# Three spacing constants and the place of the background work changed in a hybrid attention, convolution and pooling trunk on one core

## The chip, the cores and the metric

The kernel runs on one core of one Trainium2 chip. The metric is device time in microseconds (us); lower is better. A time is that of one execution; where several runs are given, the median counts.

## The reference, cut to what matters

One layer over a sequence of 2048 tokens with 1024 channels, in float32:

```
h   = rmsnorm(x) * g1;  p = h @ W_in
A   = banded attention: 8 heads x 64, chunks of 64 tokens, each with the 8 chunks before it,
      q and k normalised per head, a learned bias by clipped distance, softmax
B   = gb * conv3_causal(gc * hin)                 (256 channels)
C   = (mean over the last 2/4/8/16 tokens - u), a 64x64 map per group, a scale   (256 channels)
x   = x + concat(A, B, C) @ W_out
h2  = rmsnorm(x) * g2
x   = x + relu(h2 @ W1)^2 @ W2                    (4096 hidden)
```

## The kernel before

The tokens are worked in four blocks of 512 (`block(b)`), and after them comes the MLP over two halves of 1024 tokens, which the change does not touch. A float32 product is made of three TensorE passes (`mm3`, lines 179 to 182) over a high and a low part of each operand; the parts of a weight tile are made by `Weights.split` (cast on ScalarE or GpSimd, rest on VectorE, lines 160 and 161). All loads and stores are issued by SyncE (SP).

A block has these stages in this order on TensorE:

- `project(0)`, `project(1)`, `project(2)`: q, k and v. Each has eight steps `k` of 12 matmuls. `project(0)` also loads the block's x (`load_x`) and the rows for the first norm (`row_power`, into tiles tagged `sv`, four buffers, squared by `look_rows`). Within `project(2)`, at the steps listed in `EARLY`, k is normalised and the first pair of heads is prepared by `prep(0)`: transposes, splits, a store of k to memory (`kd`) and loads of `kx`, `qs` and `qx` for each head, partly from on-chip memory to on-chip memory. The first scores of the attention (lines 601 and 602) need these loads.
- the attention, woven with side work. `weave` takes `attention` as its main stream and a side stream. A main step is half of a unit (a head and 128 queries): either the scores, or the transposes of one unit and the values of another. There are 68 main steps. After each main step `RATE` side steps fall due (`RATE0` in block 0). The first thing that `attention` yields is `LEAD`, before any instruction of its own, so that about `LEAD * RATE` side steps stand before the first scores.

The side stream (`side`) is the output projection of the block before (`outproj`, 32 steps of 6 matmuls; eight output groups of 4 steps), and then the convolution and pooling (`convpool`, 32 steps, also 6 matmuls each, in groups `dense(g)` of 4 steps that each fill one of the two PSUM banks tagged `d`). Block 0 has only the latter. Into the first steps of `convpool` are set those of `stats`, the second norm of the block before: `token_cols` sums the squares per token after three steps, then some steps pass, then `rsqrt_steps` (11 small VectorE operations, lines 200 to 207) and `row_bcast` (line 256: eight matmul passes into a bank tagged `d`, which spread the result over all partitions), a copy and a store to `r2d`.

A third, background stream is `chores`: first `survey`, 64 steps, each of which loads two tiles of 256 KB of the MLP's weights into `sv` buffers and squares two earlier ones on ScalarE; then, from block 3's `project(1)` on, `early_operands`, 28 steps, which load x of the first two blocks from memory (`x2d`), scale it, form sums, cast it and store it (`xd`). One chore step is taken at set places of the projections, and `CHORES[b]` of one per side step (`pace`).

The order of TensorE's instructions within a weave is fixed as written (`InOrder`). The order on the other engines and on SP's queue is chosen when the kernel is built, by a planner that goes by its own estimates of times, by order in the program and by free buffers; instructions of `attention` go before others of the same neighbourhood (`AHEAD`). An engine works through its list in that order, and waits where the next one is not ready.

Of the kernel before, what the change touches and what calls it, by code (L numbers as in the profile page):

```python
# [33 lines left out]

C_G1, C_G2, C_QG, C_KG, C_CW, C_PS, C_FB = 0, 8, 16, 17, 18, 24, 26
NCOL = 34
RATE, RATE0 = 0.95, 0.45
AHEAD = 1500
GAP = 0.0
AHEADW = 2  # L40
# [1 line left out]
RAWN = 3  # L42
TK, TY = 't', 't'
ORDERED = ("PE",)
LEAD = 2
EARLY = (0, 3, 5, 6)
WIN = (2, 4, 8, 16)
SPILLS = (6, 10, 14, 18)
# [44 lines left out]
def trunk(ctx, tc, xT, xN, cols, cinv, w_qkv, w_cp, w_out, w1, w1t, w2, nbias, pool_w, outT):  # L93
# [16 lines left out]
    def pd(name, tag="d"):  # L110
        if tag == "d":
            return psd.tile([P, 512], F32, tag="d", name=name)
        return psa.tile([P, 512], F32, tag=tag, bufs=3 if tag == "t" else 1, name=name)

    def pbig(name, tag):
        return psa.tile([P, 2, 512], F32, tag=tag, bufs=1, name=name)
# [26 lines left out]
    class Weights:  # L143
# [20 lines left out]
        def next(self):  # L164
            while len(self.ready) <= min(self.used, AHEADW):
                if not self.raws:
                    self.load()
                if not self.raws:
                    break
                self.split()  # L170
                while len(self.raws) < min(self.used + 1, RAWN):
                    n = len(self.raws)
                    self.load()
                    if len(self.raws) == n:
                        break
            self.used += 1
            return self.ready.pop(0)

    def mm3(out, ah, al, bh, bl, start, stop):
        te.matmul(out, ah, bh, start=start, stop=False)  # L180
        te.matmul(out, ah, bl, start=False, stop=False)  # L181
        anchor.append(te.matmul(out, al, bh, start=False, stop=stop).ins.name)  # L182
# [15 lines left out]
    def rsqrt_steps(pool, a, n, tag):  # L198
        h = pool.tile([P, n], I32, tag=tag + "h", name=tag + "h")
        ve.tensor_scalar(h, a.bitcast(I32), 1, None, op0=ALU.arith_shift_right)  # L200
        r = pool.tile([P, n], F32, tag=tag + "r", name=tag + "r")
        ve.tensor_scalar(r.bitcast(I32), h, -1, 0x5F3759DF, op0=ALU.mult, op1=ALU.add)
        t = pool.tile([P, n], F32, tag=tag + "t", name=tag + "t")
        for _ in range(3):
            ve.scalar_tensor_tensor(out=t, in0=r, scalar=-0.5, in1=r, op0=ALU.mult, op1=ALU.mult)
            ve.tensor_tensor(out=t, in0=t, in1=a, op=ALU.mult)
            ve.scalar_tensor_tensor(out=r, in0=t, scalar=1.5, in1=r, op0=ALU.add, op1=ALU.mult)
        return r
# [36 lines left out]
    def token_cols(acc, name):  # L245
        t = pd(name)
        for i in range(NT):
            te.matmul(t[:, i : i + 1], acc[:, i * P : (i + 1) * P], ones, start=True, stop=True)
        c = sm.tile([P, NT], F32, tag="ms", name=name + "c")
        ve.tensor_scalar(c, t[:, :NT], 1.0 / D, EPS, op0=ALU.mult, op1=ALU.add)  # L250
        return c

    def row_bcast(cs, name):
        t = pd(name)
        for i in range(NT):
            te.matmul(t[:, i * P : (i + 1) * P], cs[:, i : i + 1].broadcast_to([P, P]), ident, start=True, stop=True)
        return t
# [14 lines left out]
    def value_norms(k):  # L272
        raw = scr.tile([P, 512], F32, tag="x", bufs=3, name=f"vw{k}")
        sy.dma_start(raw, w_qkv[2, k])
        g = col[:, C_G1 + k : C_G1 + k + 1]
        q = vacc if k == 0 else scr.tile([P, TB + 16], F32, tag="win", bufs=2, name=f"vq{k}")[:, :TB]
        sc.activation(q, raw, AF.Square, scale=g)
        if k:
            gp.tensor_tensor(out=vacc, in0=vacc, in1=q, op=ALU.add)
# [152 lines left out]
    def block(b, prev_out):  # L432
# [3 lines left out]
        def load_x(k):  # L436
            xr = scr.tile([P, 512], F32, tag="x", bufs=3, name=f"x{b}_{k}")
            sy.dma_start(xr, xT[k * P : (k + 1) * P, t0 : t0 + TB])
            g = col[:, C_G1 + k : C_G1 + k + 1]
            xg = xgs[k]  # L440
            sc.activation(xg[:, 0], xr, AF.Copy, scale=g)
            ve.scalar_tensor_tensor(out=xg[:, 1], in0=xr, scalar=g, in1=xg[:, 0].bitcast(F32), op0=ALU.mult, op1=ALU.subtract)
# [3 lines left out]
        def row_power(n):  # L446
            raw = scr.tile([P, 512], F32, tag="sv", bufs=4, name=f"xn{b}_{n}")
            sy.dma_start(raw, xN[4 * b + n // 2, n % 2])
            return n, raw

        def look_rows(n, raw):
            sc.activation(raw, raw, AF.Square, accum_out=sx[:, n // 2, n % 2 : n % 2 + 1])
# [4 lines left out]
        def project(c, also=lambda k: None):  # L457
            if c != 1:
                big = pbig(f"a{b}_{c}", "s")
                ac = [big[:, 0], big[:, 1]] + [pd(f"a{b}_{c}_{i}", "t") for i in range(2)]  # L460
            else:
                ac = [pd(f"a{b}_{c}_{i}", "dydt"[i]) for i in range(4)]
            rows = []
            for k in range(KT):
                if c == 0:
                    load_x(k)
                if c == 0:
                    rows.append(row_power(k))
                    if k > 1:
                        look_rows(*rows.pop(0))  # L470
                w = weights.next()
                if b == 0 and c == 1:
                    value_norms(k)
                for i in range(NT):
                    mm3(ac[i], xgs[k][:, 0, i * P : (i + 1) * P], xgs[k][:, 1, i * P : (i + 1) * P], w[:, 0, 0], w[:, 1, 0], k == 0, k == KT - 1)
                also(k)
                if b and c and k % 2:
                    next(chore, None)
            for r in rows:
                look_rows(*r)  # L480
            return ac

        acq = project(0)
        rstd, epsq = [], sm.tile([P, NT], F32, tag="epsq", name=f"epsq{b}")

# [71 lines left out]
        if b == NB - 1:  # L557
            early_open.append(True)
        ack = project(1)
        nrm["q"] = normalize(acq, "q")  # L560
        if b == 0:
# [9 lines left out]

        steps = early()
        acv = project(2, lambda k: next(steps) if k in EARLY else None)
        R = p1.tile([P, TB], F32, tag="acc", name=f"R{b}")
        vr = sm.tile([P, NT], F32, tag="vr", name=f"vr{b}")
# [77 lines left out]
        def attention(first):  # L653
            ready = first
            yield LEAD if b else LEAD * RATE / RATE0
            scored = flipped = done = None
# [148 lines left out]
        def stats():  # L805
            for _ in range(3):
                yield
            ms2 = token_cols(acc2, f"ms2_{b}")
            for _ in range(4):
                yield  # L810
            r2 = rsqrt_steps(sm, ms2, NT, "r1")
            rb2 = row_bcast(r2, f"rb2{b}")
            r2s = po.tile([P, 512], F32, tag="sq", bufs=1, name=f"r2s{b}")
            sc.copy(r2s, rb2)
            sy.dma_start(r2d[b], r2s)
            yield
# [244 lines left out]
    for n, u in enumerate(units):  # L1061
        kind, tb, c, i = u
# [86 lines left out]
```

## Time and profile before

| what | value |
|---|---|
| median of 3 runs | 2141.82 us (2135.64 to 2143.37) |
| the profiled execution | 2138.21 us |
| its span, from the first to the last instruction | 2136.3 us |
| TensorE (PE) busy | 2041.8 us, 96% of the span |
| VectorE (DVE) busy | 1337.3 us, 63% |
| ScalarE (ACT) busy | 1016.4 us, 48% |
| GpSimd (POOL) busy | 575.8 us, 27% |
| moved by DMA | 399.69 MB, mean 187 GB/s |

TensorE is busy for nearly the whole span; the other engines are not. The stages up to the MLP take about the first 960 us. Matmul ends are modelled, so what is sure in the profile is when TensorE stands idle and what ended the wait. The granted clock (PEclk) has two levels in this profile: 1.0 is 2.4 GHz, 0.5 is 1.2 GHz.

In the rows further down, a row of busy time by stretch holds the stretch and its length, then the busy time (and number of instructions) of PE, PEld, DVE, ACT and POOL, the granted clock, the busy share of the DMA engines and GB/s. A row of a timeline holds start, duration, engine, line, operation and tiles, and in brackets how long the engine stood idle before it, and what ended that.

### The profile page before, as it was taken

The page shows a single profiled execution, that of the slowest core. Times are in us where ns is not written, and L with a number is a line of the kernel's source. Part 1 is how long each engine was busy: PE and PEld are TensorE (multiplying, and loading weights), DVE is VectorE, ACT ScalarE, POOL GpSimd, SP SyncE. Part 2 cuts the span into 40 slices and gives each one's busy share as a digit, 9 for nine tenths or more (in the row PEclk, how much of TensorE's full clock was granted, in tenths as well). Part 3 has the DMA queues.
Part 4 walks back from the last instruction along what each step waited for, and adds up shares of the span by engine and source line. Part 5 has one row for each costly group of instructions (what it writes and reads, how often), then busy time and mean ns, then how long its engine had stood idle before and what let it go on. Part 6 is the DMA issues. An engine that isn't in the chain of part 4 may idle for free. (4 is left out here: it accounts for less than half of the span.)

```text
span 2136.3 us, 31619 instructions
## 1 busy us (share of the span) xinstructions
PE 2041.8 (96%) x11072; PEld 1257.2 (59%) x11072; DVE 1337.3 (63%) x2208; ACT 1016.4 (48%) x2028; POOL 575.8 (27%) x441
## 2 busy tenths in 40 slices
PE   8999898999999898998999999999999999999999
PEld 6777787887787687764444444444444444444444
DVE  6676466756676677767768779767743053353354
ACT  5466575666564454535656456456143151150330
POOL 1110012000210133154556456446422031130132
PEclk9999999999999999999999999999999999999999
DMA  9676797668854687493465555548733333333344
GB/s 318 195 226 210 225 276 238 203 219 265 269 177 124 194 263 209 156 340 115 166 228 186 182 198 187 183 148 295 250 121 104 101 102 104 99 99 107 101 151 150
DMA packets 219567, 399.69 MB, mean 187 GB/s; under 512 B 26000, under 2 KB 33296, under 8 KB 219408
## 3 DMA queue, kind: packets, MB, share of 16 engines
q1 hardware_dynamic: 219408, 397.68, 58.0%
q8 instruction: 87, 1.43, 0.3%
q14 instruction: 72, 0.59, 0.1%
HBM read 275.42 MB, written 105.38 MB: 178 GB/s over the span
## 5 line engine op out<-in xcount | busy, mean ns | idle before, releaser
L911 PE MATMUL b_d<-ft_u,s_d 128*128 128x512 f16 x1152 | 264.1, 379 | 7.3 <-ACT ft_u L861 3.2
L911 PEld LDWEIGHTS <-s_d 128*128 128x128 f16 x1536 | 150.2, 98 | 188.6 <-issue 7.3
L911 PEld LDWEIGHTS <-s_u 128*128 128x128 f16 x1536 | 150.7, 98 | 186.1 <-issue 6.8
L911 PE MATMUL b_u<-zt,s_u 128*128 128x512 f16 x1152 | 257.2, 381 | 1.5 <-DVE u2u L1014 0.8
L1032 DVE TENSOR_TENSOR acc<-acc,b_d 128x512 f32<-128x512 f32 x176 | 119.1, 682 | 178.8 <-PE b_d L911 175.6
L911 PEld LDWEIGHTS <-a_u 128*128 128x128 f16 x1152 | 112.8, 98 | 144.6 <-issue 11.4
L911 PEld LDWEIGHTS <-a_d 128*128 128x128 f16 x1152 | 112.6, 98 | 144.8 <-issue 9.8
L911 PE MATMUL b_d<-fb_u,a_d 128*128 128x512 f16 x768 | 183.7, 379 | 4.2 <-DVE acc L1032 2.0
L911 PE MATMUL b_u<-zb,a_u 128*128 128x512 f16 x768 | 176.7, 379 | 1.3 <-ACT u2u L1001 1.3
L611 ACT ACTIVATE sb<-sb,nm 128x640 f32<-128x640 f32 (+4 forms) x128 | 97.5, 762 | 143.2 <-DVE nm L605 135.2
L895 POOL TENSOR_TENSOR t1u<-u2u,c11u 128x512 f32<-128x512 f32 x32 | 43.7, 1366 | 443.4 <-ACT u2u L1018 443.4
L181 PE MATMUL a<-wq,xg 128*128 128x512 f32 x384 | 153.2, 399 | 0.5 <-DVE wq L161 0.4
L180 PE MATMUL a<-wq,xg 128*128 128x512 f32 x384 | 145.0, 402 | 8.5 <-ACT wq L160 8.5
L182 PE MATMUL a<-wq,xg 128*128 128x512 f32 x384 | 152.8, 399 | 0.0
L243 POOL TENSOR_TENSOR acc<-acc,sq 128x512 f32<-128x512 f32 x28 | 37.6, 1342 | 366.2 <-ACT sq L242 351.6
L605 DVE CUSTOM_DVE_ANT_0 sb<-s,b 128x640 f32<-128x640 f32 (+4 forms) x128 | 94.1, 735 | 66.5 <-PE s L602 65.8
L624 DVE SCALAR_TENSOR_TENSOR pp<-pt,pp 128x384 f16<-128x384 f32 (+1 forms) x224 | 104.0, 484 | 44.5 <-ACT pp L623 44.0
L180 PE MATMUL o<-mix,wo 128*128 128x512 f32 x256 | 107.3, 420 | 0.5 <-DVE gb L760 0.5
L180 PE MATMUL cp<-xg,wc 128*128 128x512 f32 x256 | 107.5, 420 | 0.0
L161 DVE TENSOR_TENSOR wq<-rwq,wq 128x512 fp32r<-128x512 f32 x96 | 68.0, 715 | 62.7 <-ACT wq L160 62.7
L623 ACT ACTIVATE pp<-pt 128x384 f16<-128x384 f32 (+1 forms) x224 | 90.8, 430 | 33.3 <-PE pt L622 32.7
L182 PE MATMUL o<-mix,wo 128*128 128x512 f32 x256 | 102.4, 400 | 0.0
(273 smaller groups left out, 4289.8 us busy)
## 6 DMA issues: line engine op xcount, KB each, us to landing
rwq<-w_qkv SPq DMA_DIRECT2D x96, 256.0 KB, 2.9
p<-w1t SPq DMA_DIRECT2D x64, 256.0 KB, 4.1
rwc<-w_cp SPq DMA_DIRECT2D x64, 256.0 KB, 4.3
rwo<-w_out SPq DMA_DIRECT2D x64, 256.0 KB, 4.2
t<-w SPq DMA_DIRECT2D x64, 256.0 KB, 3.8
r_u<-w SPq DMA_DIRECT2D x64, 256.0 KB, 3.0
wd<-s_u SPq DMA_DIRECT2D x64, 256.0 KB, 2.3
r_d<-w SPq DMA_DIRECT2D x64, 256.0 KB, 2.9
```

Source lines behind the costliest of these rows:

```text
L161: behind(ve.tensor_tensor(out=w[:, 1], in0=raw, in1=w[:, 0].bitcast(F32), op=ALU.subtract))
L180: te.matmul(out, ah, bh, start=start, stop=False)
L181: te.matmul(out, ah, bl, start=False, stop=False)
L182: anchor.append(te.matmul(out, al, bh, start=False, stop=stop).ins.name)
L243: gp.tensor_tensor(out=acc, in0=acc, in1=q, op=ALU.add)
L605: ve.tensor_tensor_reduce(out=sb[:, :nk].rearrange("p (e k) -> p e k", e=ne), in0=s[:, :ne, :hk], in1=bi[:, 640 - nk :].rearrange("p (e k) ...
L611: sc.activation(sb[:, :nk], sb[:, :nk], AF.Exp, bias=nmx, scale=-1.0, accum_out=st["l"][:, i, j : j + 1])
L623: sc.activation(pp[:, 0, c0:c1], pt[:, :n], AF.Copy, scale=PSC)
L624: ve.scalar_tensor_tensor(out=pp[:, 1, c0:c1], in0=pt[:, :n], scalar=PSC, in1=pp[:, 0, c0:c1], op0=ALU.mult, op1=ALU.subtract)
L895: gp.tensor_tensor(out=t1, in0=b12, in1=b11, op=ALU.subtract)
L911: te.matmul(bank, w[:, a, q * P : (q + 1) * P], xs[q][:, c], start=start and q == 0 and i == 0, stop=q == n - 1 and i == 2, skip_group_che ...
L1032: ve.tensor_tensor(out=a, in0=a, in1=bk, op=ALU.add)
```

## The change

Four things are set differently:

- In `project`, a chore step used to be taken after the odd steps of `project(1)` and `project(2)` (eight per block, in blocks 1 to 3). Now it is taken after steps 4 to 7 of `project(0)` and steps 0 to 4 of `project(1)` (nine per block), and none in `project(2)`. In block 3 the four of `project(0)` do nothing, because `early_operands` is let go only ahead of `project(1)`.
- `LEAD` goes from 2 to 5: before the first scores of a block stand four side steps (5 x 0.91 = 4.55) and not one (2 x 0.95 = 1.9).
- `RATE` goes from 0.95 to 0.91 and `RATE0` from 0.45 to 0.43.
- In `stats` nine steps and not four pass between `token_cols` and `rsqrt_steps` with `row_bcast`.

```
-RATE, RATE0 = 0.95, 0.45
+RATE, RATE0 = 0.91, 0.43
...
-LEAD = 2
+LEAD = 5
...
-                if b and c and k % 2:
+                if b and (c == 0 and k > 3 or c == 1 and k < 5):
                     next(chore, None)
...
             ms2 = token_cols(acc2, f"ms2_{b}")
-            for _ in range(4):
+            for _ in range(9):
                 yield
             r2 = rsqrt_steps(sm, ms2, NT, "r1")
             rb2 = row_bcast(r2, f"rb2{b}")
```

## Rows read from the trace of the kernel before

**Rows 1.** Busy time by stage: weaves of blocks 0, 1, 3; two projections of block 2.

```profile
81.00:175.00 94.00, 84.84 (x625) 70.73 (x623) 70.59 (x176) 59.57 (x157) 15.35 (x19) 0.98 0.75 224
253.00:411.00 158.00, 152.55 (x1197) 132.17 (x1196) 110.29 (x231) 103.04 (x261) 26.66 (x29) 0.98 0.77 238
411.00:434.00 23.00, 22.63 (x112) 17.91 (x111) 11.40 (x25) 15.02 (x33) 0.00 (x0) 1.00 0.80 261
434.00:456.00 22.00, 22.00 (x96) 17.61 (x95) 14.79 (x32) 14.06 (x33) 0.00 (x0) 1.00 0.64 214
726.00:905.00 179.00, 167.76 (x1267) 141.97 (x1268) 138.50 (x279) 92.53 (x201) 46.26 (x43) 0.98 0.66 199
```

**Rows 2.** TensorE's waits, whole run: total us, times, longest.

```profile
PE s L601 <- DMA qs<-qlo: 18.3, 3, 8.9
PE rb L256 <- DVE r1r L207: 12.4, 4, 4.1
...
PE y L637 <- DVE pp L624: 5.5, 8, 1.3
```

**Rows 3.** Timeline of TensorE: each block's first scores (start, us, idle before).

```profile
85.97 0.30 PE L601 MATMUL s<-kx,qs 128*128 128x128 f32 x1 [3.02 <-DMA qs<-qlo]
...
252.19 0.60 PE L601 MATMUL s<-kx,qs 128*128 128x320 f32 x1 [6.36 <-DMA qs<-qlo]
...
485.22 0.38 PE L601 MATMUL s<-kx,qs 128*128 128x320 f32 x1 [4.19 <-DMA qx<-qlo]
...
725.90 0.60 PE L601 MATMUL s<-kx,qs 128*128 128x320 f32 x1 [8.92 <-DMA qs<-qlo]
```

**Rows 4.** Busy time by stretch at half clock: after first scores, after a broadcast.

```profile
86.30:89.70 3.40, 3.22 (x9) 2.67 (x10) 0.30 (x2) 0.50 (x2) 0.04 (x1) 0.50 0.85 266
252.20:257.00 4.80, 4.80 (x13) 4.03 (x14) 1.55 (x4) 1.54 (x3) 0.00 (x0) 0.50 0.83 257
485.70:489.10 3.40, 3.40 (x10) 2.83 (x11) 1.44 (x3) 0.92 (x2) 0.00 (x0) 0.50 0.98 323
725.90:731.40 5.50, 5.50 (x15) 4.52 (x16) 3.45 (x6) 1.54 (x3) 0.00 (x0) 0.50 0.39 110
348.90:352.60 3.70, 3.67 (x13) 3.29 (x14) 1.65 (x4) 1.47 (x3) 0.00 (x0) 0.54 0.93 242
```

**Rows 5.** Timeline of SP, blocks 1 and 3: chore loads ahead of the qs loads.

```profile
240.51 1.22 SPq L306 DMA_DIRECT2D p<-w1t  x2
...
243.79 0.53 SPq L545 DMA_DIRECT2D qs<-qlo  x1
...
715.97 0.90 SPq L370 DMA_DIRECT2D e<-x2d  x2
```

**Rows 6.** Timeline of TensorE: the second norm's broadcast in blocks 1, 2, 3.

```profile
348.93 1.90 PE L256 MATMUL rb<-ident,r1r 128*128 128x128 f32 x8 [4.06 <-DVE r1r L207]
...
581.39 2.08 PE L256 MATMUL rb<-ident,r1r 128*128 128x128 f32 x8 [3.11 <-DVE r1r L207]
...
827.55 1.16 PE L256 MATMUL rb<-ident,r1r 128*128 128x128 f32 x8 [2.41 <-DVE r1r L207]
```

**Rows 7.** Timeline of VectorE around the broadcast: block 1, last row block 2.

```profile
333.52 0.15 DVE L250 TENSOR_SCALAR ms_0c<-ms 128x4 f32<-128x4 f32 x1
...
335.42 0.16 DVE L200 TENSOR_SCALAR r1h<-ms_0c 128x4 int32<-128x4 int32 x1
...
346.24 0.75 DVE L526 SCALAR_TENSOR_TENSOR qlo<-tq,qgs,qhi 128x512 fp32r<-128x512 f32 x1 [3.81 <-DMA kd<-khi]
...
348.79 0.41 DVE L624 SCALAR_TENSOR_TENSOR pp<-pt,pp 128x256 f16<-128x256 f32 x1
...
581.25 0.41 DVE L624 SCALAR_TENSOR_TENSOR pp<-pt,pp 128x256 f16<-128x256 f32 x1
```

**Rows 8.** Instructions of line 744: duration ns min/median/max, first and last start.

```profile
L744 DVE TENSOR_TENSOR hs<-cp,R x8: 679/692/692, 118.1 to 870.8; 128x512 f32<-128x512 f32 x8
```

**Rows 9.** SP's own waits, 176 to 260 us: total us, times, longest.

```profile
SPq L306 <- ACT p L302: 10.6, 7, 2.8
```

## The prediction

> **What bounds the kernel now.** I read the page first: TensorE is busy for 96% of the span, so only its idle time (2136.3 - 2041.8 = 94.5 us) and stretches at half clock can be won, and work that is merely moved on another engine is worth nothing by itself. TensorE's waits over the whole run come next: the largest is that of the first scores for the loads of `qs`, 18.3 us in three waits, and the next that of a broadcast for `rsqrt_steps`, 12.4 us in four [rows 2]. The timeline puts them in place. Every block's attention begins with a wait: 3.02, 6.36, 4.19 and 8.92 us, 22.5 us in all [rows 3], and in blocks 1 to 3 the broadcast of the second norm waits 4.06, 3.11 and 2.41 us, 9.6 us in all [rows 6]; the fourth broadcast, the other 2.8 us, stands after the last output projection, where no step is left to set between, and stays. The granted clock shows a second cost: after each of the four first waits TensorE works at half clock, for 3.2, 4.8, 3.4 and 5.5 us of busy time, and after the first broadcast for 3.67 us, after the second for a like stretch [rows 4]. Elsewhere the weaves are nearly full: block 1's has 152.55 us of 158 busy, and 4.06 of the rest is its broadcast [rows 1].
>
> **The lead.** Three more side steps ahead of the first scores are 18 matmuls; 96 matmuls of a projection take 22.00 us [rows 1], 0.23 each, so 4.2 us. They are not added, only taken earlier, out of a fixed number. Their casts, and in blocks 1 to 3 one add, one square and one store of an output group, come along; VectorE and ScalarE stand free there, because both wait for the same scores, and the store is issued when the first head's `qs` are already queued. So the lead alone turns idle time into work: 3.0, 4.2, 4.2 and 4.2 us, 15.6 us.
>
> **No chores in the third projection.** What is left is 2.2 us in block 1 and 4.7 us in block 3. In block 1 two loads of a chore (2 x 256 KB) are issued at 240.51, ahead of `qs<-qlo` at 243.79, and in block 3 two of `early_operands` at 715.97 stand right ahead of the `qs` loads [rows 5]. By their count block 1's pair is the weave's first chore, loaded as soon as the squares of `project(2)`'s chores free its buffers; with these chores gone it is loaded a projection earlier. At the 238 GB/s of block 1's weave [rows 1] 512 KB are 2.2 us. I take 2.2 us in each: block 1's wait goes wholly, 2.5 us stay in block 3. Bounds: 0 if the planner puts other loads in the same place, and all 6.9 us, since chores also hold up ScalarE's casts of k ahead of these loads. Idle time won with the lead: 15.6 + 4.4 = 20.0 us (15.6 to 22.5).
>
> **The clock.** At half speed half of the busy time is lost: (3.2 + 4.8 + 3.4 + 5.5) / 2 = 8.4 us [rows 4]. Without a wait in blocks 0 to 2 nothing lets the clock fall there; in block 3 the 2.5 us left lie by the 2.41 us after which the third broadcast's work ran on at full clock, so I take all 8.4. Lower bound 3.3: blocks 0 and 2 alone.
>
> **The broadcast.** `rsqrt_steps` moves along with it in the program, but VectorE does not wait for the program's place: the sums are there at 333.52 and the first step runs at 335.42, 1.9 us later, while TensorE reaches the broadcast at 344.87 [rows 6, 7]. Five side steps later are some 5 / 0.91 = 5.5 main steps of 158 / 68 = 2.3 us [rows 1], 12.8 us, more than any of the waits, so the broadcast itself no longer waits. But what is late next? In block 1 VectorE stood still for 3.81 us before `qlo`, behind a store of k, and the values' operand `pp` is done only at 349.20 [rows 7]. TensorE without the broadcast would do 6 matmuls (1.4 us) and five transposes (at the broadcast's 1.16 / 8 = 0.15 us a pass [rows 6], 0.7 us) and stand before the values at 347.0: 2.2 us of the 4.06 come back. In block 2 `pp` is done at 581.66 and TensorE would be there at 578.28 + 2.1 = 580.4: 1.3 of 3.11 come back. Block 3 has no such row. Won: 9.6 - 3.5 = 6.1 us, and the half clock of block 2 (3.67 / 2 = 1.8); block 1's I leave in place. New wait: the broadcast now falls exactly between the third and fourth group of `convpool`. It takes the one free `d` bank, so the fourth group's first matmul needs the bank that `hs` is reading, 0.69 us of VectorE [rows 8], with the broadcast's own 1.2 us [rows 6] between. I take 0.5 us a block, since `hs` may stand behind one other operation. Sum 6.1 + 1.8 - 1.5 = 6.4 us; bounds 0 and 9.6 + 3.7 = 13.3.
>
> **What it costs.** The lead is paid for by the rates. Main steps without a side step behind them go from 5% to 9% in three weaves and from 55% to 57% in block 0: 3 x 2.7 + 1.4, about ten more. In block 0 about 37 such steps go with 94.0 - 84.8 - 3.0 = 6.2 us of idle time besides the first wait [rows 1], 0.17 us each: 1.7 us. Upper bound 1.3 us each, the longest wait for `pp` [rows 2], 13 us. Three more steps of `early_operands` fall into block 3's weave; that weave with 20 of them has 11.2 us idle, block 1's with survey steps 5.4 [rows 1], so 0.3 us each, 0.9 us. The chores set into `project(0)` of blocks 1 and 2 add 8 x 256 KB = 2.1 MB to a stretch that moves 261 GB/s at a busy share of 0.80, so could move 326 [rows 1]: 6.0 + 2.1 MB take 24.8 us of 23.0, and 1.8 us run over into `project(1)`, which has room (0.64). TensorE never waits there now, tiles being loaded some steps ahead: I take 0 and keep 3.6 us as the bound. [...] In block 3 these four chores do nothing. The total of chores stays enough: all 64 survey steps are still done before block 3, and 28 early steps need 5 + 23 / 0.4 = 58 of 64 side steps.
>
> **Sum.** 20.0 + 8.4 + 6.4 - 1.7 - 0.9 = 32.2 us from the profiled execution's 2138.2, that is 2106.0. The median of the runs shown lies 3.6 us above that execution, so I forecast 2110 us. What a measurement here can tell from no change is about 0.5%, 10.7 us.
>
> **Rivals.** (a) The waits move on: the planner fills the freed places of SP's queue with other loads and the attention meets VectorE's late `pp` in place of the broadcast. Then only the lead's 15.6 and the clock of blocks 0 and 2 (3.3) are won, less 2.6: 16.3 us, 2125 us. For it: VectorE's stop of 3.81 us has nothing to do with the broadcast [rows 7]. Against it: no survey load is due in the stretch any more.
>
> (b) The filler is missed. If each of ten more bare main steps costs 1.3 us, (a) shrinks by 11.3 to 5.0 us, 2137 us, no change. Block 0's 0.17 us speaks against it.
>
> (c) The short stops cost the clock. If each of the ten brings a half-clock stretch like that after block 2's first scores, 3.4 us [rows 4], 1.7 us are lost each time, 17 us: 2127 us. Block 0, with 37 bare steps, keeps 0.98 of the clock, and the stretch after its first wait accounts for that [rows 1, 4], so I give it little. The Trainium skill (TensorE: Matmul & The Clock Gate, section A second HAM failure mode: psum-queue depth-cycling) tells of a kernel whose clock swung because TensorE idled shortly and often between groups; block 0's row doesn't bear it out here.
>
> (d) Slower: SP stands before a survey load in `project(0)`, where these loads now share four buffers with the row loads, and the weights queued behind it come late, so that TensorE waits in the projections. The place is steps 4 to 7 of `project(0)` and 0 to 4 of `project(1)`, blocks 1 and 2, 18 chores. The longest such stop of SP now is 2.8 us, 10.6 us in seven stops [rows 9], all hidden. From 32.2 / 18 = 1.8 us of unhidden stop per chore the gain is gone; at 2.8 each it would be 50 us, net 18 us slower, 2160 us. Against it: that cover of several tiles, and `project(1)`, busy for 22.00 of 22.00 us with four chores inside [rows 1].
>
> (e) The broadcast's change does nothing, because the chain is run as late as the program has it: 6.4 us less won, 2116 us; the 1.9 us of rows 7 speak against it.
>
> **Chances.** Forecast 0.54, (a) 0.17, (b) 0.11, (c) 0.03, (d) 0.08, (e) 0.07. Faster by over 0.5% are the forecast, (a), (c) and (e), 0.81; the same, (b), 0.11; slower, (d), 0.08. All upper bounds of the gains together give 22.5 + 8.4 + 13.3 - 2.6 = 41.6 us, 2100; with 2 us for the spread of a median the range begins at 2098. It ends at 2131, (a) with half of (b)'s loss, and leaves out (b) and (d).
>
> **What would show it.** Right: the first scores of blocks 0 to 2 follow 24 side matmuls without a wait, and block 3's waits under 3 us; the clock stays at 1.0 there; the broadcasts in blocks 1 to 3 wait for nothing, and instead a short wait for `pp` stands near. Between `kx` and `qs` SP issues no chore load. Wrong: waits for `wq` or `x` in `project(0)`, many waits of about a microsecond at the values or scores, or first scores that still wait over 3 us because the `qs` loads land later than before. A difference in the MLP would come from the planner's order, which I can't foresee; I put it at nothing.

## The result and the profile after

The changed kernel took 2113.55 us (median of four runs, 2110.28 to 2115.69) beside 2138.73 for the kernel before (2129.74 to 2143.37): a ratio of 0.9886 with a 95% interval of 0.9848 to 0.9924, 24.4 us less. The forecast was 2110. Measured again later it gave 2117.48 beside 2138.4, 0.9902 (0.9878 to 0.9927), 20.9 us less; the two agree. Its profiled execution took 2115.69 us with a span of 2113.9, 22.4 less than before.

TensorE's timeline of the changed kernel, each block's first scores, then the second norm's broadcast in blocks 1 to 3 and the fourth one:

```profile
86.48 0.22 PE L601 MATMUL s<-kx,qs 128*128 128x128 f32 x1
...
252.83 0.31 PE L601 MATMUL s<-kx,qs 128*128 128x320 f32 x1
...
477.13 0.31 PE L601 MATMUL s<-kx,qs 128*128 128x320 f32 x1
...
707.33 0.31 PE L601 MATMUL s<-kx,qs 128*128 128x320 f32 x1
...
351.04 1.05 PE L256 MATMUL rb<-ident,r1r 128*128 128x128 f32 x8
...
575.93 1.05 PE L256 MATMUL rb<-ident,r1r 128*128 128x128 f32 x8
...
812.51 1.05 PE L256 MATMUL rb<-ident,r1r 128*128 128x128 f32 x8
...
942.06 1.71 PE L256 MATMUL rb<-ident,r1r 128*128 128x128 f32 x8 [2.06 <-DVE r1r L207]
```

The four first waits of [rows 3] are gone, block 3's too, and so are the three of [rows 6]; a scores matmul takes 0.31 us where it took 0.60 at half clock. That is 22.5 + 9.6 = 32.1 us of idle time, but the span of the profiled execution fell by 22.4. TensorE's waits in the changed kernel, whole run (in total, times, longest), show part of what came in their place:

```profile
PE y L637 <- DVE pp L624: 7.5, 9, 2.2
PE pt L622 <- ACT sb L611: 5.0, 5, 2.5
...
PE y L637 <- ACT pp L623: 3.5, 2, 2.4
...
PE cp L180 <- DVE hs L744: 3.1, 2, 2.7
PE cp L180 <- DVE ms_2c L250: 2.6, 1, 2.6
PE rb L256 <- DVE r1r L207: 2.1, 1, 2.1
```

Busy time by stretch of the changed kernel (columns: window, its length, TensorE, its weight loads, VectorE, ScalarE, GpSimd, granted clock, DMA share, GB/s): weaves of blocks 0 and 1, two projections of block 2, the weave of block 3, then half-clock stretches in the weaves of blocks 0, 2 and 3, and last the MLP:

```profile
81.00:174.00 93.00, 83.99 (x612) 69.83 (x611) 71.19 (x177) 60.93 (x164) 15.04 (x18) 1.00 0.78 235
...
244.00:405.00 161.00, 158.24 (x1251) 135.90 (x1250) 117.95 (x243) 111.54 (x275) 26.65 (x29) 1.00 0.84 252
405.00:428.00 23.00, 23.00 (x102) 18.61 (x101) 7.46 (x12) 16.32 (x42) 0.00 (x0) 1.00 0.84 287
428.00:450.00 22.00, 21.12 (x88) 16.22 (x88) 12.94 (x35) 15.16 (x38) 0.00 (x0) 1.00 0.73 243
...
706.00:880.00 174.00, 163.76 (x1261) 138.20 (x1259) 144.58 (x281) 93.79 (x203) 46.53 (x43) 0.99 0.70 219
...
177.90:184.70 6.80, 5.57 (x24) 4.55 (x25) 2.87 (x5) 1.38 (x3) 0.00 (x0) 0.50 0.39 117
580.70:584.10 3.40, 3.40 (x25) 2.88 (x24) 1.66 (x10) 2.90 (x6) 0.00 (x0) 0.50 0.80 231
788.90:792.30 3.40, 3.40 (x14) 2.91 (x13) 3.37 (x5) 1.61 (x3) 3.32 (x4) 0.50 0.61 193
...
942.00:2113.90 1171.90, 1143.48 (x5252) 515.66 (x5252) 680.50 (x843) 465.12 (x777) 413.39 (x282) 0.99 0.47 153
```

Block 1 is the change at its best: 158.24 of 161 us busy at full clock. `project(0)` of block 2 with its new chores is busy for 23.00 of 23.00 us while it moves 287 GB/s, so TensorE pays nothing for the chores there. Half-clock stretches now stand behind other waits: behind the last units of block 0, and behind the two waits for `hs` and `ms_2c`.

I added up the idle times of TensorE's timeline by place and the half-clock losses of the windows, for both profiled executions. Predicted beside measured, us:

```
                                        before  after  change  predicted
first scores, blocks 0 to 3               22.5    0.0   -22.5     -20.0
broadcasts, blocks 1 to 3                  9.6    0.0    -9.6      -9.6
other waits, block 0's weave to block 3's 24.1   34.7   +10.6      +7.6   (3.5 + 1.5 + 1.7 + 0.9)
lost to half clock ahead of the MLP       13.6    6.2    -7.4     -10.2   (8.4 + 1.8)
last broadcast to the end (MLP)         1167.6 1171.8    +4.2       0
the rest, by difference                                  +2.3       0
span                                    2136.3 2113.9   -22.4     -32.2
```

Of the 10.6 us, 4.7 are in block 0's weave, 1.4, 2.6 and 1.4 in those of blocks 1 to 3, and 0.5 in the projections between them.

The MLP's part is mostly clock: its 5252 matmuls are busy for 1143.48 us, and in the kernel before for 1140.61; the stretches at half clock there hold 12.9 us of busy time, before 6.5, so that 3.2 us more are lost to them. Counted from the last broadcast's start, in the kernel before:

```profile
968.70:2136.30 1167.60, 1140.61 (x5252) 514.58 (x5252) 683.78 (x842) 464.98 (x777) 414.92 (x282) 1.00 0.47 154
```

The code of that part is the same. In the profiles of the other kernels below it took 1166.8 to 1174.3 us; why a half-clock stretch falls where it does there stays open.

### The profile page after: what moved, and what is told of

Read it like the earlier page. It is cut to its first block, busy times and chain, and to the rows that moved or that the text cites. A ratio compares the mean times of both kernels' runs of the same rounds, so it can differ in the third digit from the quotient of the medians.

```text
span 2113.9 us, 31622 instructions
## 1 busy us (share of the span) xinstructions
PE 2040.6 (97%) x11072; PEld 1253.7 (59%) x11072; DVE 1339.8 (63%) x2208; ACT 1015.3 (48%) x2028; POOL 575.9 (27%) x441
## 4 chain that ended last, share of the span: by engine, by line
PE 68%; DVE 10%; DMA 9%; ACT 5%; POOL 4%; issue 4%; SPq 1%; POOLq 0%; DVEq 0%; ACTq 0%
PE b_d L911 21%; PE b_u L911 18%; PE a L181 4%; PE a L180 4%; PE a L182 3%; PE o L180 2%; PE o L181 2%; PE o L182 2%; PE pt L622 2%; PE cp L180 2%; DMA xn<-xN 2%; PE cp L182 2%; PE cp L181 2%; DMA r_d<-w 1%; PE y L637 1%
## 5 line engine op out<-in xcount | busy, mean ns | idle before, releaser
L180 PE MATMUL o<-mix,wo 128*128 128x512 f32 x256 | 104.9, 411 | 0.8 <-ACT mix L703 0.4
L1001 ACT COPY u2u<-b_u 128x512 f32<-128x512 f32 x32 | 18.5, 577 | 175.2 <-PE b_u L911 172.1
```

## The experiments

My theory was that of the prediction: the lead covers the first scores' loads, the chores' place only the little that the lead leaves, and the broadcast's waits are mostly won. Its rivals: each part only moves its wait to the next late operand, and the parts do not add up. Behind the result a second question came up: do the waits at `hs` and `ms_2c` come from the place of a PSUM bank, as I had priced one such wait, or from a late ScalarE?

### One part alone

`e1_lead`, the kernel before with the lead:

```diff
-RATE, RATE0 = 0.95, 0.45
+RATE, RATE0 = 0.91, 0.43
-LEAD = 2
+LEAD = 5
```

> The kernel before with the lead and the two rates of the changed one; chores and broadcast as before. Theory 1 (the lead covers what its 18 matmuls last, 4.2 us, and the chores' loads account for the rest): first waits of 0, about 2.2, 0 and about 4.7 us in blocks 0 to 3, broadcasts still wait for some 9 us, 15 to 18 us faster than before. Rival 2 (the lead alone covers everything, the chores do not matter): all four first waits gone, 25 us faster. Rival 3 (the chores' loads are the cause and the lead adds nothing): first waits of 3 us and more in all of blocks 1 to 3, under 8 us faster.

`e2_chores`, the kernel before with the chores' place:

```diff
-                if b and c and k % 2:
+                if b and (c == 0 and k > 3 or c == 1 and k < 5):
```

> The kernel before with the chores taken out of the third projection alone. Theory 1: first waits shrink by some 2 us in blocks 1 and 2 and by 2 to 5 us in block 3, and stay above 2 us in three of the four blocks, half-clock stretches stay, 5 to 9 us faster. Rival 2: no first wait shrinks by more than 1 us, no change. Rival 3: first waits of blocks 1 to 3 go to nothing, 20 us faster.

`e3_bcast`, the kernel before with the broadcast five side steps later:

```diff
-            for _ in range(4):
+            for _ in range(9):
```

> The kernel before with the broadcast five side steps later alone. Theory 1 (6 us won, part of the wait comes back as a wait for the values' operand or for the bank of the third dense group): the broadcasts of blocks 1 to 3 wait for nothing, first waits as before, new waits of some 3 to 5 us close by, 4 to 8 us faster. Rival 4 (the wait only changes its name): new waits of 8 us and more within some 15 us behind, within 3 us of before. Rival 5 (the whole wait is won): 11 to 13 us faster.

Measured: the lead 2123.28 beside 2139.99, 0.9919 (0.9900 to 0.9938); the chores 2131.45, 0.9952 (0.9935 to 0.9969); the broadcast 2132.39, 0.9956 (0.9941 to 0.9972). Each alone is faster, by 17.3, 10.3 and 9.4 us. The lead's time is what theory 1 expected; the chores and the broadcast gave more than the 9 and 8 us at which their ranges ended, with intervals (6.6 to 13.9, 6.0 to 12.6 us) that reach into them, and the broadcast's leaves rival 5 open. Their sum, 37, is more than the 21 to 24 of all together. The timelines say why. TensorE with the lead alone, first scores of blocks 1 and 3:

```profile
257.05 0.38 PE L601 MATMUL s<-kx,qs 128*128 128x320 f32 x1 [2.52 <-DMA qx<-qlo]
...
711.65 0.38 PE L601 MATMUL s<-kx,qs 128*128 128x320 f32 x1 [4.14 <-DVE xo L800]
```

2.52 and 4.14 us are left, as the prediction had it (2.2 and 4.7); in block 3 the view names a VectorE operation that these scores do not read, so that the loads end the wait there is not shown. One expectation missed: the broadcasts were to wait some 9 us still, and only block 3's does, 2.87. TensorE with the chores alone, first scores of all four blocks:

```profile
85.09 0.30 PE L601 MATMUL s<-kx,qs 128*128 128x128 f32 x1 [2.50 <-DMA qs<-qlo]
...
248.18 0.38 PE L601 MATMUL s<-kx,qs 128*128 128x320 f32 x1 [2.59 <-DMA qs<-qhi]
...
478.98 0.39 PE L601 MATMUL s<-kx,qs 128*128 128x320 f32 x1 [2.07 <-DMA qs<-qhi]
...
713.40 0.38 PE L601 MATMUL s<-kx,qs 128*128 128x320 f32 x1 [2.23 <-issue]
```

Block 3's wait shrinks from 8.92 to 2.23 us, block 1's from 6.36 to 2.59, all four from 22.5 to 9.4. So the chores' place costs these loads much more than the two transfers right ahead of them; the lead and the chores' place cover the same idle time, and can be won only once. With the broadcast alone the first scores wait as before (block 3's 7.53), while the three broadcasts wait for nothing. Near them 1.52 us come back at the transposes before the values of block 1 (for `pp`), and in block 2 the wait at `tq` ahead of the broadcast grows from 2.12 to 3.36 us, 2.8 in all where theory 1 had 3 to 5. TensorE, its timeline:

```profile
354.95 1.14 PE L256 MATMUL rb<-ident,r1r 128*128 128x128 f32 x8
...
586.78 1.14 PE L256 MATMUL rb<-ident,r1r 128*128 128x128 f32 x8
...
717.97 0.61 PE L601 MATMUL s<-kx,qs 128*128 128x320 f32 x1 [7.53 <-DMA qx<-qlo]
...
828.52 1.14 PE L256 MATMUL rb<-ident,r1r 128*128 128x128 f32 x8
```

### One part undone

`e5_lead_chores` is the changed kernel with `range(4)`, `e4_lead_bcast` the changed kernel with `if b and c and k % 2:`, and `r_after` the changed kernel itself, once more.

> The changed kernel with the broadcast where it was before. Theory 1: no first wait left in blocks 0 to 2, under 3 us in block 3, broadcasts wait for some 9 us again, 22 to 28 us faster than before, so 4 to 8 us slower than the changed kernel's 24.4. Rival 4: as fast as the changed kernel within 3 us.

> The changed kernel with the chores back in the second and third projection. Theory 1, with the sizes of the runs so far (the lead covers 4.2 us of each first wait; the chores' loads are worth 4 to 7 us in blocks 1 and 3): first waits of about 2.5 us in block 1 and 4 us in block 3 come back, 6 to 11 us slower than the changed kernel. Rival 2 (with the lead the chores no longer matter): within 3 us of the changed kernel.

> The changed kernel once more, so that the next three stand beside it on the same chip: 24 us faster than before, give or take 4.

Measured: without the broadcast's part 2121.84 beside 2139.99, 0.9915 (0.9902 to 0.9929); without the chores' part 2118.84 beside 2138.4, 0.9913 (0.9888 to 0.9939), on the chip on which the changed kernel gave 0.9902 (0.9878 to 0.9927). So on top of the lead the chores are worth 1.4 us between medians, which the intervals do not tell from nothing: rival 2 and not theory 1's 6 to 11 us, though the profile of that kernel shows block 3 waiting again (and block 1 for 1.00 us):

```profile
713.04 0.60 PE L601 MATMUL s<-kx,qs 128*128 128x320 f32 x1 [4.32 <-DVE e L375]
```

With the lead and the chores but the broadcast early, the gain is 18.2 us where 22 to 28 were expected, and of the broadcasts, which were to wait some 9 us, only block 3's does (3.30 us); the lead by itself had already shifted TensorE against `rsqrt_steps` in blocks 1 and 2. What the broadcast adds to the other two, and what both add to the lead (0.9919 alone, 0.9886 and 0.9902 for the whole change, with intervals that overlap), is more than these runs can tell. The lead's gain is shown; that the other two parts add to it is not.

### The rates alone

`e8_rate`, the kernel before with 0.91 and 0.43, and `LEAD` left at 2: ten more bare main steps, and no lead.

> The kernel before with the two rates of the changed one alone (lead, chores, broadcast as before). Theory 1 (a bare main step costs 0.17 us, ten more of them): 0 to 3 us slower, block 0's weave no worse than by 1 us. Rival 6 (bare steps are what made block 0's weave 4.7 us worse in the runs with the lead): block 0's waits at the values grow by 3 us and more here too. If they do not, the lead itself is what is paid back there, because the side work runs out before the attention does.

2141.0 beside 2139.72, 1.0013 (0.9998 to 1.0029): ten more bare main steps cost nothing that is clear of noise, and by the interval at most 6 us. Block 0's weave waits 8.6 us besides its first scores, before 8.0, so rival 6 falls. Its timeline on TensorE (transposes of blocks 1 and 2), and a row of VectorE's ahead of the first, show a wait moving:

```profile
346.17 0.75 DVE L526 SCALAR_TENSOR_TENSOR qlo<-tq,qgs,qhi 128x512 fp32r<-128x512 f32 x1 [3.44 <-DMA kd<-khi]
...
347.07 0.52 PE L622 MATMUL pt<-ident,sb 128*128 128x128 f32 x3 [2.43 <-DVE r1r L207]
348.67 0.69 PE L622 MATMUL pt<-ident,sb 128*128 128x128 f32 x2 [1.08 <-DVE pp L624]
...
579.99 0.52 PE L622 MATMUL pt<-ident,sb 128*128 128x128 f32 x3 [2.49 <-DVE r1r L207]
```

The broadcast no longer waits in blocks 1 and 2 (4.06 and 3.11 us in [rows 6]), but the transposes beside it wait 3.51 and 3.57 us. In block 1 VectorE stands 3.44 us behind a store of k, as it did in [rows 7], and both `r1r` and `pp` come after that. Here rival (a)'s mechanism is at work: 7.2 us of waits have become 7.1 at other operands.

### Block 0 as before

`e7_block0_old`, the changed kernel with block 0's rate and lead as they were:

```diff
-RATE, RATE0 = 0.91, 0.43
+RATE, RATE0 = 0.91, 0.45
-            yield LEAD if b else LEAD * RATE / RATE0
+            yield LEAD if b else 2 * 0.95 / RATE0
```

> The changed kernel with block 0 paced as before (one side step ahead of the first scores, 0.45 a main step), blocks 1 to 3 as changed. If the longer lead pays in block 0 as well (3 us of waiting and 1.6 us of half clock won, next to nothing lost): 3 to 5 us slower than the changed kernel. Rival: the lead is paid back in block 0 itself, whose side steps run out earlier and leave the last main steps bare; the waits of 1 to 2.4 us at the values and the half-clock stretch at its end go, and the time is within 2 us of the changed kernel's or faster.

2114.41 beside 2138.4, 0.9887 (0.9861 to 0.9913): no different from the changed kernel, as the rival had it. Its first scores wait 2.93 us again, and the later waits of that weave fall from 11.7 (in the repeated profile) to 7.7 us, with no half-clock stretch at its end. In block 0 the lead is worth nothing that shows: it only moves the idle time from the weave's front to its end, where the side work runs out earlier.

### The waits for hs and ms_2c

One row of the changed kernel stands where I had put 0.5 us a block: that of `hs` in block 2. In blocks 1 and 3 the fourth group's first matmul waits for nothing. The row of `ms_2c` in block 3 stands 24 us ahead of that block's broadcast, at the second group: its first matmul needs the bank of `token_cols` (line 248), which `ms_2c` reads. The sum had no term for it, and the expectation of `e10_hold` below is mistaken in calling it the fourth group's. TensorE, its timeline:

```profile
568.40 0.77 PE L622 MATMUL pt<-ident,sb 128*128 128x128 f32 x5 [2.46 <-ACT sb L611]
...
579.72 0.47 PE L180 MATMUL cp<-xg,wc 128*128 128x512 f32 x1 [2.74 <-DVE hs L744]
...
782.19 0.94 PE L248 MATMUL ms<-ones,acc 128*128 128x1 f32 x8
...
788.18 0.50 PE L180 MATMUL cp<-xg,wc 128*128 128x512 f32 x1 [2.57 <-DVE ms_2c L250]
```

VectorE, its timeline at the same places:

```profile
578.09 0.89 DVE L624 SCALAR_TENSOR_TENSOR pp<-pt,pp 128x384 f16<-128x384 f32 x2 [4.80 <-ACT pp L623]
578.90 0.68 DVE L744 TENSOR_TENSOR hs<-cp,R 128x512 f32<-128x512 f32 x1
...
787.36 0.69 DVE L382 TENSOR_TENSOR eb<-e,eb 128x512 f16<-128x512 f32 x1 [4.14 <-ACT eb L381]
787.97 0.15 DVE L250 TENSOR_SCALAR ms_2c<-ms 128x4 f32<-128x4 f32 x1
```

ScalarE, its timeline:

```profile
565.79 0.63 ACT L452 ACTIVATE xn<-xn 128x512 f32<-128x512 f32 x1 [4.14 <-DMA xn<-xN]
...
574.89 0.63 ACT L452 ACTIVATE xn<-xn 128x512 f32<-128x512 f32 x1 [3.19 <-DMA xn<-xN]
...
577.59 0.74 ACT L623 ACTIVATE pp<-pt 128x384 f16<-128x384 f32 x2
...
786.71 0.62 ACT L381 CAST eb<-e 128x512 f16<-128x512 f32 x1 [4.89 <-DMA xd<-eb]
```

Read from the bottom up: ScalarE stands 3.19 us before the square of a row of the *next* block's x, whose load has not come; the cast of `pp` (line 623) is queued behind it, with two more squares and an exponential between; VectorE stands 4.80 us for that cast with `hs` queued behind, and TensorE stands 2.74 us for the bank that `hs` reads. At 565.79 the same, with 4.14 us of ScalarE and 2.46 of TensorE, and at 786.71 a cast of `early_operands` whose buffer a store still holds: VectorE stands 4.14 us for it, with `ms_2c` behind. These squares stood in block 2's weave before, too (4.9 us of ScalarE in two waits, from 598.6 on); they now come some 33 us earlier (the weave itself begins 8 us earlier), beside the broadcast.

`e6_bcast7`, the changed kernel with `range(7)`: the broadcast then falls in the middle of a group, not on the boundary between two.

> The changed kernel with seven steps and not nine ahead of the broadcast, so that it falls in the middle of the third dense group and not between the third and the fourth. If the broadcast's place costs through the PSUM bank that the third group still holds: the 2.7 us wait for the third group's gate operation in block 2 goes, 2 to 5 us faster than the changed kernel. Rival: that wait came from ScalarE, which stood for 3 to 4 us behind a load of rows, and so VectorE was late anyhow; then a wait of 2 us or more stays there under another name, and the time is within 2 us of the changed kernel's.

`e11_rows_behind`, the changed kernel with the row squares tied to their place in the program, by the helper that already ties the survey's squares (line 302):

```diff
-            sc.activation(raw, raw, AF.Square, accum_out=sx[:, n // 2, n % 2 : n % 2 + 1])
+            behind(sc.activation(raw, raw, AF.Square, accum_out=sx[:, n // 2, n % 2 : n % 2 + 1]))
```

> The changed kernel with the squares of the rows for the first norm held behind the matmuls of the first projection, so that the planner can't set them into the weave of the block before. If ScalarE's stops of 3 to 4 us behind the loads of these rows make block 2's waits (2 to 2.7 us for the third group's gate operation, 2 to 2.5 us at the transposes): both waits and the half-clock stretch go, 3 to 6 us faster than the changed kernel. Rival: the bank of the third group is what counts, and the wait for it stays at 2 us or more.

`e10_hold`, the changed kernel with no `early_operands` step in block 3's side steps 28 to 37:

```diff
-CHORES = (0.3, 0.36, 0.36, 0.4)
+CHORES = (0.3, 0.36, 0.36, 0.46)
-            for _ in steps:
-                due += CHORES[b]
+            for n, _ in enumerate(steps):
+                due += 0.0 if b == 3 and 28 <= n < 38 else CHORES[b]
```

> The changed kernel with no chore step taken in block 3 from side step 29 to 38, around the sums of the second norm, and 0.46 and not 0.40 a step elsewhere in that block. If ScalarE's stop of 4 to 5 us behind a store of the early operands is what makes the fourth-group wait of 2.5 us in block 3: that wait and the half-clock stretch behind it go, 2 to 4 us faster than the changed kernel, unless the denser chores make other waits. Rival: the wait comes from VectorE's own load and stays at 2 us or more.

Measured: `e6_bcast7` 2116.94 beside 2138.4, 0.9891 (0.9864 to 0.9917), no different from the changed kernel. The wait at `hs` is gone from block 2, as the bank would have it, but TensorE waits there as long as before, 9.6 us in all besides the first scores (8.1 and 8.9 in the two profiles of the changed kernel). The longest waits of blocks 2 and 3:

```profile
571.45 0.90 PE L622 MATMUL pt<-ident,sb 128*128 128x128 f32 x3 [3.42 <-ACT sb L611]
...
791.64 0.80 PE L180 MATMUL cp<-xg,wc 128*128 128x512 f32 x1 [4.02 <-DVE ms_2c L250]
```

And `e7_block0_old`, with the broadcast on the boundary, waits 0.5 us at `hs`. So the broadcast's place among the banks decides under which name TensorE meets the late operand, and does not make it late. The Trainium skill (Perfetto Trace Analysis, section Matmuls) advises that independent groups of matmuls rotate through different PSUM banks, so that one group's drain overlaps the next group's matmuls. The two banks here do rotate; the rows of `hs` and `ms_2c` show drains that are late for another reason, and moving the group in between leaves 3.42 us at `sb`.

`e11_rows_behind` 2106.92 beside 2139.72 (2104.57 to 2109.2), 0.9846 (0.9829 to 0.9862): faster than the changed kernel too. All its five runs lie under the ten of the changed kernel (lowest 2110.28), which did not stand beside them on the same chip; its interval stands clear of the repeated measurement's (0.9878 to 0.9927) and overlaps the first one's (0.9848 to 0.9924) a little. TensorE's waits in its block 2, 465 to 635 us, come to 4.3 us, and the largest are:

```profile
PE s L601 <- DVE nm L605: 2.0, 2, 1.1
PE yt L649 <- DVE yn L643: 1.4, 1, 1.4
PE pt L622 <- DVE pp L624: 0.8, 2, 0.5
```

Waits for `hs` and `sb` are gone from it. The squares of block 3's rows now run from 627.8 us, at the end of that weave, and stand behind no load there. Block 2's waits fall from 8.9 to 4.3 us and block 0's from 11.7 to 8.7 against the repeated profile of the changed kernel; block 1's grow from 2.8 to 4.7. In block 3, which has no next block's rows, the wait at `ms_2c` stays (2.96 us). Of the 10.0 us between these two profiles 6.4 lie ahead of the last broadcast; the other 3.6 are in the MLP, which this line does not touch.

`e10_hold` 2116.97 beside 2139.72, 0.9892 (0.9875 to 0.9909): no gain. Its wait at `ms_2c` is gone, but 2.76 us at `hs` in block 2 stay, and in block 3 a scores matmul waits 2.12 us for `nm`; that weave's waits are 9.9 us as against 10.6. One late cast was taken away, and TensorE waits nearly as long for other operands.

`e12_all` puts `e10_hold`, `e11_rows_behind` and `e7_block0_old` together.

> Both of the last two and block 0 paced as before. If the three causes are separate: 5 to 9 us faster than the changed kernel, some 27 to 31 us faster than before. If waits only move on: within 3 us of the changed kernel.

2108.79 (2096.74 to 2113.74), 0.9845 (0.9821 to 0.9869): inside the range expected for separate causes, but nothing over `e11_rows_behind`, which beats both kernels with one line changed on top of the change.

I did not try a third buffer for the casts of `early_operands` (tag `pg`); whether it would take away block 3's wait for a store stays open.

## Why the prediction came out right, point by point

**What bounds it, and the lead.** Right. The time was in TensorE's idle time ahead of the first scores, and filler that stood in the stream anyway took it; `e1_lead` leaves 2.52 and 4.14 us where 2.2 and 4.7 were worked out, and is 17.3 us faster. Only in block 0 did the 3.0 us come back at the weave's end (`e7_block0_old`).

**No chores in the third projection.** The mechanism was right: in the changed kernel SP issues one weight load between `kx` and `qs` of block 1, and no chore. SP, its timeline, for [rows 5]:

```profile
240.43 0.97 SPq L540 DMA_DIRECT2D kx<-kd  x2
241.99 0.33 SPq L154 DMA_DIRECT2D rwo<-w_out  x1
243.40 0.48 SPq L545 DMA_DIRECT2D qs<-qhi  x1
```

The term was too small: I counted two transfers, 2.2 us in block 3, and alone this part takes 6.7 us from block 3's wait and 13.1 from the four. So no 2.5 us stayed in block 3. In time that hardly shows, since the lead covers most of the same idle time.

**The clock.** 7.4 us of the 10.2 came. The half-clock stretches of the first scores are gone as forecast; new ones of 6.8, 3.4 and 3.4 us stand behind the end of block 0 and behind the waits at `hs` and `ms_2c`. What I missed is that a wait which comes back can bring its half clock with it. Not each does: behind 2.46 us at 568.40 TensorE goes on at full clock.

**The broadcast.** That it waits for nothing was right, and so was that `rsqrt_steps` does not wait for the program's place, which was rival (e): then the waits of [rows 6] would have stayed. That 3.5 us come back was near what the broadcast alone shows (`e3_bcast`, 2.8 us, of which 1.52 for `pp`), but around block 1's broadcast, from 320 to 360 us, the changed kernel waits 0.6 us in all. The bank wait is the step that failed: 0.5 us a block, reasoned from the 0.69 us of `hs`, measured 2.74 us in block 2 (1.96 in the repeated profile) and none in blocks 1 and 3. Its reason was wrong more than its size: the bank's reader is late because ScalarE stands for a load, two engines further back, and a like stop behind a store made the wait at `ms_2c`, 2.57 us, for which I had nothing. Where I looked for what is late next I asked about VectorE, and not about ScalarE's queue.

**What it costs.** Ten more bare main steps cost at most 6 us by the interval of `e8_rate`, where rivals (b) and (c) needed 11 and 17, so both fall. But block 0 pays 4.7 us more waits where I had 1.7 for all, because its side work ends sooner. The chores in `project(0)` cost next to nothing: in block 2's projections, from 405 to 474 us, TensorE waits 0.8 us in all, and in block 1's, from 181 to 244 us, not at all, so rival (d) did not come. I had worked out that 8.1 MB fall into 23.0 us of `project(0)` and 1.8 us run over; the row shows 287 GB/s at a share of 0.84 with TensorE busy throughout, which is 6.6 MB, 0.6 more than before and not 2.1. Nor was 326 GB/s the most that can move: from 20 to 40 us the kernel before moves 376.

**The MLP**, put at nothing, took 4.2 us back, 3.2 of them by more half clock.

So the sum was 9.8 us too good on the profiled execution (32.2 against 22.4): +2.5 for the first scores, -3.0 for waits that came back, -2.8 for the clock, -4.2 for the MLP, -2.3 for the rest. Rival (a)'s mechanism is real: against the 32.1 us of idle time that went, waits at other operands grew by 10.6, though not at its two places, the loads of `qs` and the late `pp` beside the broadcast. The 24.4 us gained in the first measurement lie halfway between the forecast's 32.2 and the 16.3 of (a); the 22.4 between the profiles and the 20.9 of the second measurement lie nearer to (a).

That the time came out so near to 2110 is in part luck. The forecast was counted from 2141.82 us, the median of three runs; a fourth brought the median before to 2138.73, and from there the same sum gives 2106.5, 7 us under the measured 2113.55.

## What to carry to other kernels

Filler that stands in the stream anyway belongs ahead of the first instruction that depends on a transfer, where enough of it is left for the end (block 0 had too little); two remedies for one wait can be won once, so single-part runs must not be added up. Where a wait goes, look two engines back: list what each in-order engine has at the head of its queue at that time, and ask which of these waits for a DMA that the waiting work has nothing to do with. Work for a later stage (the next block's rows) is better tied to its place; otherwise a planner may slip it in front of work that is due now, as it did here.

## What the runs showed of the hardware beyond expectation

One square of 0.63 us on ScalarE, for a block that starts tens of microseconds later, stood at the head of its queue for a load, and three engines stopped: 3.19 us of ScalarE, 4.80 of VectorE, 2.74 of TensorE, and then 3.4 us of TensorE at 0.50 of its clock. With such squares tied to their place these waits are gone (`e11_rows_behind`), and the last broadcast comes 6.4 us earlier in the profile.

A stretch of 287 GB/s with a DMA share of 0.84 ran beside TensorE at 23.00 of 23.00 us busy, so a queue this full was no cost by itself there. It costs where TensorE waits for a transfer: with the chores taken away from ahead of the first scores' loads, their waits fell from 22.5 to 9.4 us (`e2_chores`).
